# Requesting w_xo's last loads ahead of the expert weights, and a new order of the router's steps, in a hybrid mLSTM, attention and MoE block

## The chip, the cores and the metric

The kernel runs on one core of one Trainium2 chip. Its time is the device time of one execution in microseconds, taken as the median of several runs. A profiled execution gives a trace beside it: for each engine (TensorE, called PE here, with its weight loads PEld; VectorE, DVE; ScalarE, ACT; GpSimd, POOL; SyncE, SP, which issues most DMAs) when each instruction ran and what it waited for.

## What is computed

One block of a hybrid model on 512 tokens of width 1024, all in fp32: a mixer (mLSTM heads and forgetting attention, merged through `w_out`), a cross attention to 256 memory rows, and a mixture of 32 experts in four groups of which each token takes two. The change sits where the cross attention ends and the router begins:

```python
o = jnp.einsum('bhsn,bnhd->bshd', p.astype(v.dtype), v)
x = x + o.reshape(B, S, D) @ w_xo                  # residual 2
t = rmsnorm(x, g_moe)
g_logits = t @ w_rg + b_rg                         # 4 groups
e_logits = (t @ w_re + b_re).reshape(-1, N_GROUPS, EXPERTS_PER_GROUP)
# group by argmax, two experts in it by top_k, weights by softmax
for e in range(N_EXPERTS):
    he = jax.nn.silu(t @ w_gate[e]) * (t @ w_up[e])
    y = y + combine[:, e:e + 1] * (he @ w_down[e])
x = x + y
return rmsnorm(x, g_final)
```

## The kernel before

Every fp32 product of the dense part is made of three fp32r products (`mm3`, L102 to L105): an operand is split into a high part (ScalarE's copy, `wh`, L124) and a low part (VectorE's difference, `wl`, L125). `load_w` (L111) requests 512 KB of weights on SP into one of three buffers `wraw` and emits both halves of the split.

The product with `w_xo` is made in four column blocks of 256 (`resid_rows`, L522). The first two run beside the last head of the cross attention. The last two, `rw2` and `rw3` (L663), run token block by token block in the router's stretch: `of_block(tb)` (L181) makes the 24 products of one block of 128 tokens (12 with the weights' rows 0 to 511, 12 with the rest) and VectorE adds them to the residual (L525). In the order string below such a block is called `x0` to `x3` (for `rw2`) or `p0` to `p3` (for `rw3`). Each column block needs two loads, so the stretch has four.

The router's steps have letters too, and a token block behind them. `t` turns half a token block of the residual on PE (stage 0: columns 0 to 511; stage 1: the rest) and copies it out of PSUM (`rsc`); `l` multiplies it with the router's weights (`pso`, 40 columns); `s` and `r` sum the squares (ACT, L770) and take the power on POOL (L99); `X` writes the scaled residual in two fp16 parts, the high one on ACT (L783), the low one on DVE (L784); `g` scales the logits (`lg`, L790); `C` chooses the experts for two blocks (some 14 small DVE operations, from L799 to `ab`, L820); `K` counts places in three or seven small products (L829) and a chain on DVE; `G` gathers the first pair's tokens (L885). After that the experts run in 16 pairs: gate and up (L1045), turn (L1058), down (L1069), combine (L1095).

What sets the order: on PE, DVE and ACT the string `ROUT` (L46) is followed to the letter in this stretch (`manual_schedule`, L664); each of these engines works its instructions in order. SP and POOL are not in that list; their order is made by the scheduler of the framework. Expert weights are requested in 1 MB pieces in a ring of buffers (`RING`, L42): nine `m`, one `h` and one `l` (which share the buffers of w_xo's split halves and so wait for block p3) and three `r`. `experts.load(9)` requests the first nine, `experts.load(NAHEAD)` two more.

The weights' two last loads are requested at two places: `rw3.load(0)` ahead of `experts.load(9)` (L666), `rw3.load(4)` at the string's letter `v` (L671), which stood first in it.

Of the kernel before, what the change touches and what calls it, by code (L numbers as in the profile page):

```python
# [15 lines left out]
AF = mybir.ActivationFunctionType  # L16
OP = mybir.AluOpType
# [5 lines left out]
NB = T // P  # L23
# [19 lines left out]
NAHEAD = 11  # L43


ROUT = ("v x0 t00 t01 s0 l00 p0 t02 l01 t03 s1 r0 x1 l02 t10 X0 l03 p1 l10 r1 s2 x2 t11 X1 s3 g0 l11 g1 C0 p2 r2 x3 t12 "  # L46
        "X2 K0 l12 g2 p3 t13 r3 l13 g3 C1 G0 K1 X3 G1")
NR = 8 + NE

C_MLQ, C_MLK, C_MLV, C_MLO = 0, 512, 1024, 2048  # L50
# [8 lines left out]
def emit(ctx, tc, a):  # L59
    nc = tc.nc  # L60
    V, S, G, TE, SP = nc.vector, nc.scalar, nc.gpsimd, nc.tensor, nc.sync
# [66 lines left out]
    def drain(g):  # L128
        for _ in g:
            pass  # L130
# [367 lines left out]
    X1 = [X1a[:, tb] for tb in range(NB)]  # L498
# [17 lines left out]
    r2 = ExitStack()  # L516
# [5 lines left out]
    def resid_rows(src, hs, hl_, c):  # L522
        def ev(tb, n, ps):
            x = X1a[:, tb:tb + n, c * 256:(c + 1) * 256]
            V.tensor_add(x, x, ps)  # L525
        return Rows(src, c * 256, hs, hl_, NB, ev)
# [45 lines left out]
    xh = [XH[:, k] for k in range(KB)]  # L572
    xl = [XL[:, k] for k in range(KB)]
# [89 lines left out]
    rw2, rw3 = (resid_rows(a["w_xo"], oth, otl, c) for c in (2, 3))  # L663
    with tc.manual_schedule(engines={mybir.EngineType.PE, mybir.EngineType.DVE, mybir.EngineType.Activation}):  # L664
        rw2.loads()
        rw3.ws = [rw3.load(0)]  # L666
        experts.load(9)
        for w in ROUT.split():
            n = [int(x) for x in w[1:]]
            if w == "v":  # L670
                rw3.ws.append(rw3.load(4))  # L671
                experts.load(NAHEAD)
            elif w[0] in "xp":
                drain((rw2 if w[0] == "x" else rw3).of_block(n[0]))
            else:
                router[w[0]](*n)
# [48 lines left out]
def moe(ctx, tc, a, X2, dram, small, acc, pss, pso, left, right, ident, rpow, wp, c, mraw, wx):  # L725
    nc = tc.nc
    V, S, G, TE, SP = nc.vector, nc.scalar, nc.gpsimd, nc.tensor, nc.sync
# [14 lines left out]
    sq, lgs, m8s, ids = {}, {}, {}, {}  # L742
# [4 lines left out]
    def turn(stage, tb):  # L747

        pt = pss()
        for j, k in enumerate(range(*READY[stage])):  # L750
            TE.transpose(pt[:, j * P:(j + 1) * P], X2[tb][:, k * P:(k + 1) * P], ident)
        t = tTs[stage, tb] = wx.tile([P, 4, P], F32, name="rsc", tag="rsc", bufs=2)
        ptv = pt.rearrange("p (j t) -> p j t", j=4)
        if (stage, tb) == (1, NB - 1):
            V.tensor_copy(t, ptv)
        else:
            S.activation(t, ptv, AF.Copy)

    lp = []

# [15 lines left out]
        V.tensor_scalar(v, v, 1.0 / (D * XS * XS), None, op0=OP.mult)  # L776
        sq[tb] = rpow(v)

    def parts(tb):

        xh, xl = (c.XN[:, i, tb].rearrange("p (j q) -> p j q", j=KB) for i in range(2))
        xv = X2[tb].rearrange("p (q j) -> p j q", j=KB)
        S.activation(xh, xv, AF.Copy, scale=sq[tb][:, 0:1])  # L783
        V.scalar_tensor_tensor(xl, xv, sq[tb][:, 0:1], xh, op0=OP.mult, op1=OP.subtract)  # L784

    def scaled(tb):
        h, i = tb // 2, tb % 2
# [89 lines left out]
    def first(h):  # L877
# [3 lines left out]
        for i in range(4):  # L881
            for g, pt in enumerate(c.pts):
                for j in range(4):
                    tb, k = 2 * h + i // 2, 4 * g + j
                    TE.matmul(pt[:, j * P:(j + 1) * P], c.XN[:, i % 2, tb, k * P:(k + 1) * P], c.G0[:, tb],  # L885
                              start=h + i + j == 0, stop=h == 1 and i + j == 6, skip_group_check=True)

    router = dict(G=first, X=parts, C=choose, K=place, t=turn, l=logits, s=squares, r=rstd, g=scaled)
    c.codes, c.numbers = codes, numbers
    experts = Experts(ctx, tc, a, X2, dram, small, acc, pss, pso, left, right, ident, rpow, wp, c, mraw)  # L890
# [395 lines left out]
```

## Time and profile before

| | us |
|---|---|
| median of 3 runs | 1322.14 |
| lowest and highest | 1318.31, 1324.91 |
| the profiled execution | 1318.45 |
| its span, from the first to the last instruction | 1316.7 |
| PE busy in the span | 1252.7 (95%) |
| DVE, ACT, POOL busy | 553.1, 355.1, 131.9 |
| mean granted TensorE clock | 0.984 of full speed |
| router's stretch, from the end of block x0 to the first expert product | 750 to 823 |
| experts, to the end of the last pair's gate and up | 823 to 1287 |

The profile's page gives the time that each engine is busy, the chain of work that ended last (followed back from the last instruction to whatever released it), and groups of instructions. The trace answers with rows for a stretch: a timeline of one engine (start, length, line, operation, tile, and in brackets how long the engine was idle before it and what ended that), tables of stretches, and the waits by who waited for whom. The granted clock is a share of 2.4 GHz; its lower level is 0.50, 1.2 GHz. Engine time that waits for nobody's need costs nothing, so a share of busy time over the whole span says little about one stretch.

### The profile page before, as it was taken

The page shows a single profiled execution, that of the slowest core. Times are in us where ns is not written, and L with a number is a line of the kernel's source. Part 1 is how long each engine was busy: PE and PEld are TensorE (multiplying, and loading weights), DVE is VectorE, ACT ScalarE, POOL GpSimd, SP SyncE. Part 2 cuts the span into 40 slices and gives each one's busy share as a digit, 9 for nine tenths or more (in the row PEclk, how much of TensorE's full clock was granted, in tenths as well). Part 3 has the DMA queues.
Part 4 walks back from the last instruction along what each step waited for, and adds up shares of the span by engine and source line. Part 5 has one row for each costly group of instructions (what it writes and reads, how often), then busy time and mean ns, then how long its engine had stood idle before and what let it go on. Part 6 is the DMA issues. An engine that isn't in the chain of part 4 may idle for free.

```text
span 1316.7 us, 18633 instructions
## 1 busy us (share of the span) xinstructions
PE 1252.7 (95%) x7606; PEld 902.3 (69%) x7606; DVE 553.1 (42%) x1046; ACT 355.1 (27%) x626; POOL 131.9 (10%) x250
## 2 busy tenths in 40 slices
PE   6999999999999999999999867999999999999996
PEld 5898999888888977899978756444444444444443
DVE  5436455234565645447455326232232322222225
ACT  5335344223343433326334233010000000000102
POOL 0002010000001000001000002211111221111001
PEclk9999999999999999999999977999999999999998
DMA  4343432344254225324412614899999999999981
GB/s 167 86 106 88 78 99 74 96 82 103 74 94 84 78 96 160 111 98 149 162 49 64 270 66 176 343 418 418 418 417 417 419 417 417 414 416 417 419 333 65
DMA packets 99114, 278.45 MB, mean 211 GB/s; under 512 B 6197, under 2 KB 67909, under 8 KB 77905
## 3 DMA queue, kind: packets, MB, share of 16 engines
q1 hardware_dynamic: 97536, 272.46, 57.5%
q0 software_dynamic: 1488, 4.76, 1.1%
q8 instruction: 61, 1.00, 0.3%
q14 instruction: 29, 0.23, 0.0%
HBM read 275.08 MB, written 2.12 MB: 211 GB/s over the span
## 4 chain that ended last, share of the span: by engine, by line
PE 90%; DVE 3%; DMA 3%; ACT 1%; issue 1%; SPq 0%; POOL 0%; POOLq 0%; ACTq 0%; DVEq 0%
PE acc L1045 17%; PE acc L103 16%; PE acc L105 16%; PE acc L104 16%; PE pso L1069 8%; PE pss L1020 4%; DMA wraw<-w_xo 1%; PE pss L1095 1%; PE pso L1096 1%; PE pso L1095 1%; PE pss L103 1%; PE pss L105 1%; PE pss L104 1%; PE pss L1058 1%; PE pss L1096 1%
## 5 line engine op out<-in xcount | busy, mean ns | idle before, releaser
L1045 PE MATMUL acc<-mw,st 128*64 128x512 f32 x880 | 235.8, 598 | 0.6 <-DVE st L1022 0.6
L125 DVE TENSOR_TENSOR wl<-wraw,wh 128x1024 fp32r<-128x1024 f32 x120 | 146.8, 1224 | 200.0 <-ACT wh L124 195.5
L124 ACT ACTIVATE wh<-wraw 128x1024 fp32r<-128x1024 f32 x120 | 126.8, 1058 | 209.3 <-PE acc L104 91.0
L1045 PEld LDWEIGHTS acc<-mw,st 128*64 128x64 f32 x880 | 67.2, 136 | 108.2 <-issue 102.8
L103 PE MATMUL acc<-hH,wh 128*128 128x512 f32 x320 | 127.8, 399 | 0.0
L104 PE MATMUL acc<-hL,wh 128*128 128x512 f32 x320 | 127.2, 397 | 0.0
L105 PE MATMUL acc<-hH,wl 128*128 128x512 f32 x320 | 125.3, 399 | 1.7 <-DVE wl L125 1.7
L1080 DVE SCALAR_TENSOR_TENSOR yl<-pso,wsl,yh 128x512 fp32r<-128x512 f32 x32 | 22.6, 746 | 225.3 <-ACT yh L1079 225.3
L1069 PE MATMUL pso<-mw,hT 128*64 128x512 f32 x440 | 112.6, 592 | 0.7 <-ACT hT L1060 0.7
L104 PE MATMUL acc<-wl,hH 128*128 128x256 f32 x384 | 109.1, 285 | 1.0 <-DVE wl L125 1.0
L103 PE MATMUL acc<-wh,hH 128*128 128x256 f32 x384 | 109.3, 286 | 0.5 <-ACT wh L124 0.5
L105 PE MATMUL acc<-wh,hL 128*128 128x256 f32 x384 | 109.1, 285 | 0.2 <-DVE hL L196 0.2
L1031 POOL TENSOR_SCALAR G<-iot,code 128x64 f16<-128x64 f32 x120 | 52.7, 466 | 318.0 <-PE pss L1020 312.7
L1069 PEld LDWEIGHTS pso<-mw,hT 128*64 128x64 f32 x440 | 37.2, 137 | 61.4 <-issue 59.2
L104 PEld LDWEIGHTS acc<-wl,hH 128*128 128x128 f32 x384 | 73.1, 191 | 1.9 <-DVE wl L125 1.5
L103 PEld LDWEIGHTS acc<-wh,hH 128*128 128x128 f32 x384 | 72.7, 190 | 1.3 <-ACT wh L124 0.9
L105 PEld LDWEIGHTS acc<-wh,hL 128*128 128x128 f32 x384 | 73.0, 190 | 0.5 <-DVE hL L196 0.4
L105 PEld LDWEIGHTS acc<-hH,wl 128*128 128x128 f32 x320 | 60.2, 188 | 15.8 <-DVE wl L125 2.2
L103 PEld LDWEIGHTS acc<-hH,wh 128*128 128x128 f32 x320 | 60.3, 188 | 13.3 <-ACT wh L124 0.4
L104 PEld LDWEIGHTS acc<-hL,wh 128*128 128x128 f32 x320 | 60.3, 188 | 13.2
L1020 PEld LDWEIGHTS <-xn 128*128 128x128 f16 x960 | 53.7, 98 | 22.7 <-issue 22.7
L1079 ACT ACTIVATE yh<-pso,wsl 128x512 fp32r<-128x512 f32 x32 | 20.2, 683 | 154.1 <-PE pso L1069 154.1
(321 smaller groups left out, 2352.6 us busy)
## 6 DMA issues: line engine op xcount, KB each, us to landing
mw<-w_gate SPq DMA_DIRECT2D x55, 1024.0 KB, 14.4
mw<-w_up SPq DMA_DIRECT2D x55, 1024.0 KB, 13.4
mw<-w_down SPq DMA_DIRECT2D x55, 1024.0 KB, 11.8
wraw<-w_in SPq DMA_DIRECT2D x64, 512.0 KB, 5.2
wraw<-w_xkv SPq DMA_DIRECT2D x16, 512.0 KB, 3.4
mwl<-w_gate SPq DMA_DIRECT2D x10, 512.0 KB, 10.1
mwh<-w_up SPq DMA_DIRECT2D x10, 512.0 KB, 10.5
mwh<-w_down SPq DMA_DIRECT2D x10, 512.0 KB, 11.8
```

What stands on the lines that cost most here:

```text
L103: TE.matmul(out, ah, bh, start=start, stop=False, **kw)
L104: TE.matmul(out, ah, bl, start=False, stop=False, **kw)
L105: TE.matmul(out, al, bh, start=False, stop=stop, **kw)
L124: S.activation(h, raw, AF.Copy)
L125: V.tensor_sub(l, raw, h.bitcast(F32))
L1020: TE.matmul(pt[:, j * n:(j + 1) * n], c.XN[:, i % 2, i // 2, (4 * g + j) * P:(4 * g + j + 1) * P], G_[:, i // 2, :n], start=i == 0, stop=i ...
L1031: G.tensor_scalar(G_[:, tb, i * 64:i * 64 + 64], iot[:, :64], c.code[:, tb, e:e + 1], None, op0=OP.is_equal)
L1045: TE.matmul(ps[i][half(h)], sts[k // 4][:, k % 4, half(h)], w[i][k], start=k == 0, stop=k == KB - 1)
L1069: TE.matmul(o[n][half(h)], hT[:, j, half(h)], w[j][:, n * 512:(n + 1) * 512], start=j == 0, stop=j == 3)
L1080: V.scalar_tensor_tensor(yl[:k, c], o[n][:k], wcol, yh[:k, c].bitcast(F32), op0=OP.mult, op1=OP.subtract)
L1095: TE.matmul(o, C[:k, ts], yh[:k, c], start=True, stop=False)
L1096: TE.matmul(o, C[:k, ts], yl[:k, c], start=False, stop=True)
```

## The change

All four loads of `rw2` and `rw3` are now called for ahead of `experts.load(9)`, and the letter `v` stands behind x0 and two turns and requests expert pieces alone. In `ROUT` a block of products stands between the block whose residual a turn needs and that turn, and another between a turn and its logits; the chain g0, g1, C0 stands behind p2, l11 and r2; X2 and X3 are cut in their ACT half (`h`) and their DVE half (`l`), with K0 and p3, or K1, between the halves. The copy of the last turn (`t13`), which DVE made, goes to ACT like the others.

```diff
--- before.py
+++ after.py
@@ -43,8 +43,8 @@
 NAHEAD = 11
 
 
-ROUT = ("v x0 t00 t01 s0 l00 p0 t02 l01 t03 s1 r0 x1 l02 t10 X0 l03 p1 l10 r1 s2 x2 t11 X1 s3 g0 l11 g1 C0 p2 r2 x3 t12 "
-        "X2 K0 l12 g2 p3 t13 r3 l13 g3 C1 G0 K1 X3 G1")
+ROUT = ("x0 t00 t01 v s0 p0 l00 t02 s1 r0 x1 l01 t03 X0 p1 t10 l02 s2 r1 x2 l03 l10 t11 X1 s3 p2 l11 r2 g0 g1 C0 x3 t12 "
+        "X2h K0 p3 X2l l12 t13 r3 l13 g2 g3 C1 G0 X3h K1 X3l G1")
 NR = 8 + NE
 
 C_MLQ, C_MLK, C_MLV, C_MLO = 0, 512, 1024, 2048
@@ -663,12 +663,11 @@
     rw2, rw3 = (resid_rows(a["w_xo"], oth, otl, c) for c in (2, 3))
     with tc.manual_schedule(engines={mybir.EngineType.PE, mybir.EngineType.DVE, mybir.EngineType.Activation}):
         rw2.loads()
-        rw3.ws = [rw3.load(0)]
+        rw3.loads()
         experts.load(9)
         for w in ROUT.split():
-            n = [int(x) for x in w[1:]]
+            n = [int(x) if x.isdigit() else x for x in w[1:]]
             if w == "v":
-                rw3.ws.append(rw3.load(4))
                 experts.load(NAHEAD)
             elif w[0] in "xp":
                 drain((rw2 if w[0] == "x" else rw3).of_block(n[0]))
@@ -751,10 +750,7 @@
             TE.transpose(pt[:, j * P:(j + 1) * P], X2[tb][:, k * P:(k + 1) * P], ident)
         t = tTs[stage, tb] = wx.tile([P, 4, P], F32, name="rsc", tag="rsc", bufs=2)
         ptv = pt.rearrange("p (j t) -> p j t", j=4)
-        if (stage, tb) == (1, NB - 1):
-            V.tensor_copy(t, ptv)
-        else:
-            S.activation(t, ptv, AF.Copy)
+        S.activation(t, ptv, AF.Copy)
 
     lp = []
 
@@ -776,12 +772,14 @@
         V.tensor_scalar(v, v, 1.0 / (D * XS * XS), None, op0=OP.mult)
         sq[tb] = rpow(v)
 
-    def parts(tb):
+    def parts(tb, which="hl"):
 
         xh, xl = (c.XN[:, i, tb].rearrange("p (j q) -> p j q", j=KB) for i in range(2))
         xv = X2[tb].rearrange("p (q j) -> p j q", j=KB)
-        S.activation(xh, xv, AF.Copy, scale=sq[tb][:, 0:1])
-        V.scalar_tensor_tensor(xl, xv, sq[tb][:, 0:1], xh, op0=OP.mult, op1=OP.subtract)
+        if "h" in which:
+            S.activation(xh, xv, AF.Copy, scale=sq[tb][:, 0:1])
+        if "l" in which:
+            V.scalar_tensor_tensor(xl, xv, sq[tb][:, 0:1], xh, op0=OP.mult, op1=OP.subtract)
 
     def scaled(tb):
         h, i = tb // 2, tb % 2
```

Where instructions stand in the built programs, before and after, is shown at three places.

On SP, around w_xo's last load (`wraw_7239` before, `wraw_7221` after; the `mw` are 1 MB pieces of expert weights). Before:

```order
L116 DMA wraw_7215<-w_xo 128x4x256
L931 DMA mw_7221<-w_gate 128x2048
L931 DMA mw_7223<-w_up 128x2048
L931 DMA mw_7225<-w_gate 128x2048
L931 DMA mw_7227<-w_up 128x2048
L931 DMA mw_7229<-w_up 128x2048
L931 DMA mw_7231<-w_gate 128x2048
L931 DMA mw_7233<-w_up 128x2048
L931 DMA mw_7235<-w_gate 128x2048
L931 DMA mw_7237<-w_gate 128x2048
L116 DMA wraw_7239<-w_xo 128x4x256
```

Nine pieces of the experts stand ahead of it. After, on the same engine:

```order
L116 DMA wraw_7215<-w_xo 128x4x256
L929 DMA mw_7227<-w_gate 128x2048
L929 DMA mw_7229<-w_up 128x2048
L929 DMA mw_7231<-w_gate 128x2048
L929 DMA mw_7233<-w_up 128x2048
L929 DMA mw_7235<-w_up 128x2048
L929 DMA mw_7237<-w_gate 128x2048
L116 DMA wraw_7221<-w_xo 128x4x256
L929 DMA mw_7239<-w_up 128x2048
L929 DMA mw_7241<-w_gate 128x2048
L929 DMA mw_7243<-w_gate 128x2048
```

The last w_xo load has moved up past three of the nine pieces; six are still ahead of it.

On PE, around turn t11 (`pss`) and the logits (`pso`), between the end of block x2 and the start of block p2; minus is before, plus is after:

```order
 L104 MATMUL acc<-wl,oth_5687 128x256
 L105 MATMUL acc<-wh,otl_5688 128x256
-L751 MATMUL pss<-ident,x_4532 128x128 x4
-L766 MATMUL pso<-wr,rsc 128x40 x4
+L762 MATMUL pso<-wr,rsc 128x40 x8
+L750 MATMUL pss<-ident,x_4532 128x128 x4
 L103 MATMUL acc<-wh,oth_5673 128x256
 L104 MATMUL acc<-wl,oth_5673 128x256
```

Before, t11 is followed at once by its own logits l11; after, l03 and l10 come first, then t11, and l11 stands behind the block of products.

On DVE, around the residual add of block p3 (L525), behind the last hit of K0 (`G`). Before:

```order
L735 SCALAR_TENSOR_TENSOR G_5666<-iot,cd,GA 128x128
L790 SCALAR_TENSOR_TENSOR lg<-pso,rpow,br 128x40
L525 TENSOR_TENSOR x_4532<-x_4532,acc 128x256
L755 COPY rsc<-pss 128x512
L775 TENSOR_SCALAR vv<-ss 128x1
L776 TENSOR_SCALAR vv<-vv 128x1
L790 SCALAR_TENSOR_TENSOR lg<-pso,rpow,br 128x40
```

After, at the same place:

```order
L734 SCALAR_TENSOR_TENSOR G_5666<-iot,cd,GA 128x128
L525 TENSOR_TENSOR x_4532<-x_4532,acc 128x256
L782 SCALAR_TENSOR_TENSOR xn_7195<-x_4532,rpow,xn_7195 128x1024
L771 TENSOR_SCALAR vv<-ss 128x1
L772 TENSOR_SCALAR vv<-vv 128x1
L788 SCALAR_TENSOR_TENSOR lg<-pso,rpow,br 128x40 x2
```

X2's low half (`xn`), which stood ahead of K0's chain, now stands behind p3's add; the copy of t13 has left the engine, and both scalings g2 and g3 stand together.

## Rows read from the trace of the kernel before

**Rows 1.** The page, the chain that ended last, by engine.

```profile
PE 90%; DVE 3%; DMA 3%; ACT 1%; issue 1%; SPq 0%; POOL 0%; POOLq 0%; ACTq 0%; DVEq 0%
```

**Rows 2.** The chain row by row, experts: start us, length us, what.

```profile
902.63 3.58 PE acc L1045 x16
...
932.81 3.58 PE acc L1045 x16
```

**Rows 3.** Table of stretches: us, busy PE PEld DVE ACT POOL, PEclk, DMA share, GB/s.

```profile
750.20:766.10 15.90, 1.10 (x10) 0.86 (x9) 0.49 (x1) 1.58 (x3) 0.00 (x0) 0.60 0.78 316
766.10:770.47 4.37, 4.36 (x20) 4.36 (x21) 1.06 (x2) 1.05 (x3) 0.00 (x0) 0.50 0.00 0
...
790.94:797.77 6.83, 6.82 (x32) 6.83 (x33) 2.97 (x21) 1.45 (x8) 0.00 (x0) 0.50 0.00 0
...
822.90:1287.00 464.10, 460.09 (x2770) 204.74 (x2772) 130.82 (x221) 36.88 (x60) 71.17 (x129) 1.00 0.98 403
```

**Rows 4.** The chain row by row, router's stretch.

```profile
764.52 1.06 ACT wh L124
...
786.44 2.12 ACT xn L783
788.58 2.05 DVE xn L784
...
822.90 0.64 PE acc L1045
```

**Rows 5.** Timeline of SP: start us, us, engine, line, operation, tile.

```profile
739.30 0.50 SPq L931 DMA_DIRECT2D mw<-w_gate  x1
739.85 0.49 SPq L931 DMA_DIRECT2D mw<-w_up  x1
...
742.98 0.33 SPq L931 DMA_DIRECT2D mw<-w_gate  x1
745.52 0.38 SPq L116 DMA_DIRECT2D wraw<-w_xo  x1
...
804.52 0.33 SPq L936 DMA_DIRECT2D mwl<-w_gate  x1
```

**Rows 6.** DMA issues, sixth and ninth expert piece: KB, us to landing.

```profile
mw<-w_gate SPq DMA_DIRECT2D x1, 1024.0 KB, 16.2
...
mw<-w_gate SPq DMA_DIRECT2D x1, 1024.0 KB, 20.1
```

**Rows 7.** Timeline of PE: start us, us, line, tile, [idle before <-releaser].

```profile
766.11 1.93 PE L766 MATMUL pso<-wr,rsc 128*128 128x40 f32 x8 [14.81 <-ACT rsc L757]
...
773.57 0.36 PE L103 MATMUL acc<-wh,oth 128*128 128x256 f32 x1
...
776.52 0.98 PE L766 MATMUL pso<-wr,rsc 128*128 128x40 f32 x8
777.33 0.63 PE L751 MATMUL pss<-ident,x 128*128 128x128 f32 x4
...
790.95 1.90 PE L766 MATMUL pso<-wr,rsc 128*128 128x40 f32 x8 [5.05 <-DVE lg L790]
...
802.02 1.08 PE L766 MATMUL pso<-wr,rsc 128*128 128x40 f32 x8 [0.62 <-ACT rsc L757]
...
809.25 0.44 PE L751 MATMUL pss<-ident,x 128*128 128x128 f32 x2 [2.99 <-DVE x L525]
```

**Rows 8.** Timeline of DVE: step r1, then scaling g1 and the end of C0.

```profile
784.14 0.21 DVE L775 TENSOR_SCALAR vv<-ss 128x1 f32<-128x1 f32 x1 [0.79 <-ACT xn L770]
...
792.89 0.26 DVE L790 SCALAR_TENSOR_TENSOR lg<-pso,rpow,br 128x40 f32<-128x40 f32 x1 [2.09 <-PE pso L766]
...
795.98 0.19 DVE L820 TENSOR_TENSOR ab<-eb 128x64 bf16<-128x64 bf16 x1
```

**Rows 9.** Waits of SP's queue, of PE in experts: us, times, longest.

```profile
SPq L931 <- PE acc L1045: 214.1, 52, 14.1
...
PEld acc L1045 <- DMA mw<-w_down: 1.2, 4, 0.4
```

## The prediction

> **What bounds the kernel now.** I read the page's chain of waits first: TensorE (PE) holds 90% of it [rows 1]. In the chain row by row, the experts' stretch repeats: the same step of two neighbouring pairs stands at 902.63 and 932.81 us, 30.18 us apart, and nothing but PE lies between [rows 2]. That stretch, 822.9 to 1287 us, has PE busy 460.1 of 464.1 us at full clock and moves 403 GB/s [rows 3]. The change leaves its instructions and their order alone; it can only start earlier or later. So the question is when the first expert product runs (822.90 us, [rows 4]), and the stretch to read is the router's, from 750 us on.
>
> There PE is not the bound. In the table of stretches it is busy 1.1 us of 15.9 us from 750.2 to 766.1, and after this gap the granted clock is 0.50 (1.2 GHz) until 770.47; after a second gap it is 0.50 again from 790.94 to 797.77 [rows 3]. The PE timeline says what each gap waits for: 14.81 us for ScalarE's copy (rsc) of the first turn, 5.05 us for VectorE's scaled logits (lg, L790), 0.62 us for a copy, 2.99 us for the residual add of p3 [rows 7]. The first is no fault of the copy. ScalarE works in order, and ahead of the copy stands the split of w_xo's last load, which starts at 764.52 [rows 4]. That load was issued at 745.52 behind nine 1 MB loads of expert weights [rows 5].
>
> **Part 1, the load.** The words say "ahead of the experts' loads"; the built order says otherwise. On SP the last w_xo load now stands behind six expert loads in place of nine. The sixth was issued at 739.30 and landed 16.2 us later, at 755.5; the ninth was issued at 742.98 and landed 20.1 us later, at 763.1 [rows 5, 6]. So 7.6 us separate them, 2.5 us for each MB, and landings come in the order of the requests. Before, the split began 1.4 us after the ninth landing; the same distance behind the sixth is 757.0. Bounds: 755.5 (no distance at all) and 759.5 (as late as the expert load behind it, plus the distance). I take 757.0, since both loads are of one size and shape and stand in one queue. SP issues it at about 739.9, where the seventh expert load went [rows 5]; the three expert loads that it now precedes get 0.5 MB later, and nobody needs them before 830 us.
>
> The Trainium skill (DMA: Bandwidth & Descriptors, section "Queues, rings and completion order") says that on each DMA engine requests are taken in ring order, but that completion is not first in, first out for the issuing engine. By the first half the load waits for six; by the second it could land early, which is my third rival. The landings read here are in order.
>
> With the split at 757.0 and 1.06 us long [rows 4], the high half is there at 758.1. PE meanwhile runs more than before: x0, two turns, and now half of block p0 (the 12 products of w_xo's rows 0 to 511, already split), since p0 no longer stands behind the first logits. A 24-product block takes 776.52 - 773.57 = 2.95 us at full clock [rows 7], so half is 1.5. PE resumes at 758.1, 8.0 us earlier than 766.11, with 1.5 us done; then it waits about 1.1 us for the low half on VectorE, which follows the high half. Head: 8.0 + 1.5 - 1.1 = **8.4 us** gained (bounds 6 to 10 with the landing).
>
> **Part 2, logits and turns.** (a) The 5.05 us wait stood at l11, whose PSUM tile g0 reads; g0 waited behind both halves of parts X1 (2.12 us on ScalarE from 786.44, 2.05 us on VectorE from 788.58 [rows 4]). Now l11 stands ahead of g0 and has block p2 between its turn and itself: 2.95 us cover the turn's copy. **5.05** gained. The 0.62 us in front of l12 goes for the same reason: **0.6**.
>
> (b) What is late next is K0, whose three products need the end of C0. From turn t11 on, X1 takes 0.6 (copy) + 2.1 + 2.05 us, then p2's add 0.4, r2 (0.8 until the square is there, two small operations 0.4), g0 0.2, and g1 with C0, which ran from 792.89 to 796.17, 3.3 us [rows 8]: about 10 us after t11. PE has p2, l11, x3 and t12 in that time: 2.95 + 0.8 + 2.95 + 0.5 = 7.2 us; 0.8 is 777.33 less 776.52, a set of logits [rows 7]. A new wait of about 3 us, which I take as **-3.1** with the products' way to VectorE and back. Behind it queue p3, l12 and t13.
>
> (c) The 2.99 us before t13: PE had ended p3 by 806.26 (809.25 less 2.99), yet p3's add was done only at about 809.2 [rows 7], because X2's low half and K0's chain stood ahead of it on VectorE. In the new order the low half stands behind that add, and l12 (0.8 us) covers the add's 0.4 and the way to it. The wait goes and l12 has moved under cover: **3.4** gained. In return r3's small operations stand behind X2's low half and come 0.6 to 0.9 us later into g3, and t13's copy goes to ScalarE, 0.6 us for VectorE's 0.7, which alters nothing: **-0.8**.
>
> (d) The clock. Before, 4.36 + 6.82 us of PE's work ran at 0.50 [rows 3]; at full clock it would have taken half, so 5.6 us were lost. After, the head's gap shrinks from 14.8 to 5.6 us but still is longer than the 5.05 us after which the clock fell, so the first products run at 1.2 GHz, and more of them: the rest of p0, l00, t02 and part of x1. From 758.1 I put the rise, as after the first gap (4.4 us) or the second (6.8 us), between 763 and 767; I take 7.9 us of work, 4.0 us lost. Net **+1.6**, bounds -1 and +4. Here the skill (TensorE: Matmul & The Clock Gate, "What's actually happening") adds that the activity monitor runs freely and doesn't restart with the kernel, so this term may differ from run to run; no view here can show that.
>
> **Sum.** 8.4 + 5.05 + 0.6 - 3.1 + 3.4 - 0.8 + 1.6 = 15.2 us, bounds 10 and 19. The tail behind it (C1, G0, K1, X3, G1) keeps its order on VectorE; splitting X3 and X2 in two names moves no further ScalarE work past another engine's need. Everything from 822.90 on moves along: SP waits for PE's products to free a buffer, 214.1 us in 52 waits, and PE's waits for weights are at most 0.4 us [rows 9], so the loads are released by PE and come earlier with it. The profiled execution took 1318.45 us (span 1316.7): it would be 1303.2. The median of the runs is 3.7 us higher, 1322.14, and the spread 1318.31 to 1324.91; less 15.2 that is **1307 us**.
>
> **Rivals.**
> 1. The gap at K0 drops the clock as the 5.05 us gap did. For: it is about 3 us long, with little work just ahead of it. Against: after the 2.99 us gap at 809.25 the next logits did not slow at once. Price: block p3 at half speed, at most another 2.95 us: 1310 us.
> 2. The load comes no earlier: it shares the queue with the loads behind it, and its 1 KB rows are served late. Then 7.6 us of the head stay: 1314.7 us. For: before, it was the last in the queue and had no company. Against: the landings are in order.
> 3. It does what its words say, the load landing among the w_xo loads at about 743. Then nothing waits at the head: 14.8 in place of 8.4, and no slow stretch there, 4 us more: 1297 us. Against: the built order of SP.
> 4. Slower: the experts' loads can't follow. The loads that wait for p3's products (804.52 on SP [rows 5]) precede the first expert product by 18.4 us; about 17 are left, for some 5 MB at 2.5 us each. If PE overtakes the weights, it waits in each pair, and the stretch behind each wait runs at 1.2 GHz: one 16-product stretch (3.58 us [rows 2]) in 14 pairs is 50 us, 1357 us. It decides as soon as PE's waits for weights exceed about 1 us a pair; today they are 0.4 at most, so I give it little.
>
> **How the numbers follow.** The forecast, 1304 to 1310, has 0.60; rival 1 0.15; rival 2 0.08; rival 3 0.07; rival 4 0.03; 0.07 is left for things between. The range 1300 to 1313.5 takes the forecast, rival 1, the landing's bounds and the runs' spread of some 3 us, and leaves out rivals 2, 3 and 4, 0.18 together. A difference under 0.5% (6.6 us) can't be told from no change: 0.90 faster, 0.07 the same (half of rival 2 and a forecast whose small terms all fail), 0.03 slower.
>
> **What would show it.** Right: w_xo's last split starts near 757; PE's first gap is near 5.6 us and comes inside p0, not ahead of l00; no wait of logits for lg; a new wait of some 3 us at the products of place K0; no wait of t13 for the add; the first expert product near 807.5; the pairs still 30.18 us apart. Wrong: the split near 743 or 764, a half-clock stretch behind K0, or waits for mw tiles in the experts.

## The result, and the profile after

| | before | after |
|---|---|---|
| median of 4 runs, us | 1322.31 | 1304.53 |
| lowest and highest | 1318.31, 1324.91 | 1304.21, 1306.05 |
| the profiled execution | 1318.45 | 1306.05 |
| its span | 1316.7 | 1304.3 |
| forecast | | 1307 (1300 to 1313.5) |

The ratio is 0.987, with an interval of 0.9844 to 0.9897, all of it below 1: faster, as forecast, though by less than 2%. The medians differ by 17.8 us where 15.2 were forecast. Between the two profiled executions it is 12.4. The sum was worked out on one profiled execution and subtracted from a median, so this gap between 12.4 and 17.8 has to be explained too.

The chain of the profile after, by engine, answers to [rows 1]; two rows of it, from the experts, to [rows 2] (start us, length us, what):

```profile
PE 91%; DVE 4%; DMA 2%; ACT 1%; issue 1%; SPq 1%; POOL 0%; POOLq 0%; ACTq 0%; DVEq 0%
```

```profile
890.15 3.58 PE acc L1043 x16
...
920.33 3.58 PE acc L1043 x16
```

The pairs are still 30.18 us apart. PE's waits for weights in the experts (us, times, longest) are as small as before [rows 9]:

```profile
PEld acc L1043 <- DMA mw<-w_up: 0.9, 3, 0.3
```

So from these pairs on the experts came earlier as one block (their first products did not, see below), and rival 4 (their loads can't follow) is out. The router's stretch, ScalarE and then PE (start us, us, line, tile, in brackets the idle time before and what ended it), answers to [rows 4, 7]:

```profile
757.44 1.06 ACT L124 ACTIVATE wh<-wraw 128x1024 fp32r<-128x1024 f32 x1 [13.79 <-DMA wraw<-w_xo]
```

```profile
758.55 0.58 PE L103 MATMUL acc<-wh,oth 128*128 128x256 f32 x1 [5.19 <-ACT wh L124]
759.81 0.58 PE L104 MATMUL acc<-wl,oth 128*128 128x256 f32 x1 [0.68 <-DVE wl L125]
...
789.92 0.18 PE L827 MATMUL pso<-ab,before 128*128 128x32 bf16 x1 [3.05 <-DVE ab L818]
...
792.92 0.98 PE L762 MATMUL pso<-wr,rsc 128*128 128x40 f32 x8
...
795.06 1.09 PE L762 MATMUL pso<-wr,rsc 128*128 128x40 f32 x8 [0.69 <-ACT rsc L753]
795.97 1.96 PE L883 MATMUL pss<-G,xn 128*128 128x128 f16 x32
...
800.12 0.18 PE L827 MATMUL pso<-ab,before 128*128 128x32 bf16 x1 [2.15 <-DVE ab L818]
...
803.62 2.72 PE L883 MATMUL pss<-G,xn 128*128 128x128 f16 x24 [3.22 <-DVE G L734]
806.87 1.04 PE L883 MATMUL pss<-G,xn 128*128 128x128 f16 x8 [0.52 <-DVE xn L782]
808.26 7.53 PE L1043 MATMUL acc<-mw,st 128*64 128x512 f32 x24 [0.36 <-DVE st L1020]
```

These are all of PE's waits between x0 and the experts. The split starts at 757.44, the gap comes inside p0 and is 5.19 us long, the waits for `lg` and for p3's add are gone, place K0 has its new wait of 3.05. One wait was not in the forecast: 2.15 us at place K1. The first expert product runs at 808.26, not 807.5, and with its 23 followers takes 7.53 us, where the same 24 took 5.37 before. The table of stretches (us, busy PE PEld DVE ACT POOL, granted clock, DMA share, GB/s) answers to [rows 3]:

```profile
758.55:768.20 9.65, 8.97 (x41) 8.68 (x42) 2.33 (x5) 3.35 (x9) 0.55 (x1) 0.50 0.46 192
768.20:797.97 29.77, 26.04 (x242) 25.54 (x242) 16.43 (x57) 15.16 (x27) 2.24 (x4) 1.00 0.17 54
...
803.62:808.26 4.64, 3.76 (x33) 3.23 (x32) 3.94 (x7) 0.00 (x0) 4.64 (x7) 0.50 0.97 408
```

The clock stays at 2.4 GHz over the wait at K0 and through p3, so rival 1 did not happen in this execution. It is at 1.2 GHz behind the first gap and again at 803.62, after PE had waited 2.15 and 3.22 us with little work between.

### The profile page after: what moved, and what is told of

Same layout as the page of the kernel before. It is cut to its first block, busy times and chain, and to the rows that moved or that the text cites. A ratio compares the mean times of both kernels' runs of the same rounds, so it can differ in the third digit from the quotient of the medians.

```text
span 1304.3 us, 18633 instructions
## 1 busy us (share of the span) xinstructions
PE 1253.0 (96%) x7606; PEld 900.9 (69%) x7606; DVE 552.6 (42%) x1045; ACT 355.7 (27%) x627; POOL 132.3 (10%) x250
## 4 chain that ended last, share of the span: by engine, by line
PE 91%; DVE 4%; DMA 2%; ACT 1%; issue 1%; SPq 1%; POOL 0%; POOLq 0%; ACTq 0%; DVEq 0%
PE acc L1043 18%; PE acc L103 16%; PE acc L104 16%; PE acc L105 16%; PE pso L1067 8%; PE pss L1018 4%; PE pss L1093 1%; DMA wraw<-w_xo 1%; PE pso L1094 1%; PE pso L1093 1%; PE pss L103 1%; DVE wl L125 1%; PE pss L105 1%; PE pss L104 1%; PE pss L1056 1%
```

## The experiments

### One part of the change alone

e_order keeps the new order of the steps and puts the load back behind nine pieces; e_load keeps the old order and moves the load alone.

```diff
(e_order, against the changed kernel)
-        rw3.loads()
+        rw3.ws = [rw3.load(0)]
         experts.load(9)
+        rw3.ws.append(rw3.load(4))
...
(e_load, against the kernel before)
-        rw3.ws = [rw3.load(0)]
+        rw3.loads()
...
-                rw3.ws.append(rw3.load(4))
```

> The changed kernel with one thing undone: w_xo's last load is requested behind nine expert pieces again (as before), all steps of the router stay in the new order. Theory (the two parts add up): the last split starts near 764.5 us in place of 757.4, PE's gap inside p0 grows from 5.2 to some 12.3 us, and everything behind it moves by 7.1 us: about 1311.6 us, first expert product near 815.4. Rival A (the load hardly matters, since VectorE's chain sets the end of the stretch): some of the 7.1 us come back before the first expert product, 1304 to 1307 us. Rival B (the order brings nothing without the load): about 1320 us.

> The kernel before with one thing changed: w_xo's last load is requested behind six expert pieces in place of nine, the router's steps stay in the old order. Theory: the last split starts near 757 us, PE's gap of 14.8 us shrinks by 7.5, and the waits of 5.05, 0.62 and 2.99 us stay: about 1314.7 us, first expert product near 815.4. Rival A (the load hardly matters): 1320 us or more. Rival B (the load is the whole of the change): 1305 us.

| | median, us | ratio to before, interval | saved |
|---|---|---|---|
| e_order | 1311.98 (5 runs) | 0.9933 (0.9912 to 0.9954) | 10.3 |
| e_load | 1314.80 (6 runs) | 0.9943 (0.9924 to 0.9962) | 7.5 |
| both, the change | 1304.53 (4 runs) | 0.987 (0.9844 to 0.9897) | 17.8 |

Saved is counted from 1322.31. 10.3 + 7.5 = 17.8, and both rivals of each expectation fall. That the sum is exact is chance, since the runs of e_order spread over 3.2 us and those of e_load over 5. The traces add up too: from the end of x0 (the start of turn t00) to the first expert product it is 74.11 us in a second profile of the kernel before (r_before, below), 67.12 in e_load, 64.68 in e_order and 57.37 in the changed kernel. The load alone saves 7.0, the order alone 9.4, both 16.7. The first gap of PE in the two profiles, e_order and then e_load:

```profile
763.55 0.58 PE L103 MATMUL acc<-wh,oth 128*128 128x256 f32 x1 [12.75 <-ACT wh L124]
```

```profile
758.60 1.93 PE L765 MATMUL pso<-wr,rsc 128*128 128x40 f32 x8 [7.22 <-ACT rsc L756]
```

Three expert pieces ahead of the load cost 12.75 - 5.19 = 7.6 us in the new order and 14.81 - 7.22 = 7.6 in the old, 2.5 us a piece, as read from the landings [rows 5, 6].

### The load truly first

Six pieces still stood ahead of it. SP had to wait there for one of three `wraw` buffers, and since SP's order is the framework's to make, it put expert pieces ahead; that the wait was its reason is argued, not shown. e_first holds SP to the written order.

```diff
-    with tc.manual_schedule(engines={mybir.EngineType.PE, mybir.EngineType.DVE, mybir.EngineType.Activation}):
+    with tc.manual_schedule(engines={mybir.EngineType.PE, mybir.EngineType.DVE, mybir.EngineType.Activation, mybir.EngineType.SP}):
         rw2.loads()
```

> The changed kernel, with SP's instructions held to the written order too, so that all loads of w_xo stand ahead of every expert piece; SP then waits for a buffer until about 739.4 us and requests the expert pieces some 3 us later. Theory: the load lands near 743.5 us, the gap of 5.2 + 0.7 us inside p0 goes, the stretch at 1.2 GHz from 758.5 to 768.2 (some 4.8 us lost) goes with it: 10 us less than the changed kernel, 1294 us; experts' weights still land 25 us ahead of use. Rival A: PE only reaches the wait at place K0 earlier, since VectorE's and ScalarE's chains don't get faster; that wait grows from 3 to 6 us: 1298 us. Rival B: the expert pieces that come 3 us later are missed later: PE waits for weights, 1305 us or more.

1294.66 us (4 runs), ratio 0.98 (0.9775 to 0.9825): 9.9 us less than the changed kernel, 10 expected. The load's issue (KB, us to landing), in the changed kernel and then in e_first:

```profile
wraw<-w_xo SPq DMA_DIRECT2D x1, 512.0 KB, 17.4
```

```profile
wraw<-w_xo SPq DMA_DIRECT2D x1, 512.0 KB, 3.4
```

The same half megabyte takes 17.4 us behind six pieces and 3.4 us with none ahead. SP stands still for it, and the first piece goes out later:

```profile
735.53 3.56 SPq L116 DMA_DIRECT2D wraw<-w_xo  x2
739.15 0.50 SPq L929 DMA_DIRECT2D mw<-w_gate  x1
```

That is 739.15 in place of 736.62, and its use is at 798.52; PE's waits for weights stay at 0.3 us at most, so rival B falls. Rival A falls too: the wait at K0 is 3.04 us as before. The stretches show where the 10 us were: the gaps of 5.19 and 0.68 us and 9 us of work at half speed (4.5 us lost) are gone, 10.4 us in all; p3 and the logits behind it, slower by 1.5 us, take part of it back. From x0's end to the first expert product it is 48.29 us, 9.1 less than in the changed kernel. The profiled executions differ by more, 11.9 us, mostly because the first 24 expert products took 5.37 us here.

```profile
747.56:778.80 31.24, 28.21 (x244) 28.03 (x243) 12.82 (x39) 16.38 (x28) 1.64 (x3) 1.00 0.53 222
778.80:782.96 4.16, 4.16 (x27) 4.16 (x27) 2.61 (x11) 0.99 (x7) 0.58 (x1) 0.69 0.40 92
...
784.33:798.52 14.19, 7.05 (x84) 6.21 (x82) 11.90 (x46) 5.98 (x13) 6.73 (x9) 0.76 0.92 352
```

The second row is what rival 1 of the prediction had described: behind the same wait at K0, 3.04 us, the clock did fall here, and K0's products with p3 took 4.16 us where the changed kernel had 3.0 (789.92 to 792.92).

### Single steps of the order

Three changes to the changed kernel's order string, of which the parts that move are shown; the second also gives t13's copy back to VectorE:

```diff
(e_l11)
-t11 X1 s3 p2 l11 r2 g0 g1 C0 x3 t12
+t11 X1 s3 g0 l11 g1 C0 p2 r2 x3 t12
(e_x2)
-X2h K0 p3 X2l l12
+X2 K0 p3 l12
-        S.activation(t, ptv, AF.Copy)
+        if (stage, tb) == (1, NB - 1):
+            V.tensor_copy(t, ptv)
+        else:
+            S.activation(t, ptv, AF.Copy)
(e_k0)
-X2h K0 p3 X2l l12
+X2h p3 K0 X2l l12
```

> The changed kernel with one reordering undone: l11 stands behind turn t11 and g0 again, and block p2 behind C0, as before. Theory (terms a and b of the sum): the wait of l11 for VectorE's scaled logits comes back (5.0 us) and the wait at place K0 (3.05 us) goes, so PE reaches p3 2.0 us later and all behind it too: 1306.5 us; if the clock falls behind that gap as it did in the kernel before, up to 3.4 us more. Rival A: C0, K0 and the tail come earlier by as much as p2 comes later, and the time stays at 1304.5. Rival B: the reordering was worth its 5.05 us whole: 1309.5 us.

> The changed kernel with the part on X2 and t13 undone: X2's low half stands ahead of K0's chain on VectorE again, and VectorE copies t13. By the prediction (3.4 less 0.8) this costs 2.6 us: 1307.1 us. Theory after seeing the trace: the add of p3 comes 1.4 us later and PE waits for it at t13, but r3's small operations no longer stand behind X2's low half, so the scaled logits g3, which set the end, come only some 0.8 us later: 1305.3 us. Rival: the add that comes later moves everything behind it by the 3 us that t13 waited in the kernel before: 1307.5 us.

> The changed kernel with K0's three products moved behind block p3, which fills PE's wait of 3.05 us at place K0. Theory: behind p3 VectorE's chain (add of p3, K0's chain, X2's low half, g3, C1, K1's chain, X3's low half: some 15 us of work in a row) sets the end, so PE's 3 us come back as other waits and the first expert product moves by less than 1 us: 1304 us. Rival: PE's waits add up to the end, and the time falls by the whole 3 us to 1301.5 us.

e_l11: 1306.95 us (4 runs), 2.4 more than the changed kernel, 2.0 expected. The wait of l11 is back with 5.11 us, that at K0 is gone; putting p2 ahead was worth the difference and not the 5.05 us that the row in the kernel before shows. Both rivals fall.

```profile
781.57 1.90 PE L762 MATMUL pso<-wr,rsc 128*128 128x40 f32 x8 [5.11 <-DVE lg L788]
```

In the trace the first expert product comes 51.66 us after PE's resumption, 1.95 later than the 49.71 of the changed kernel, and 5.11 - 3.05 is 2.06. The clock did fall behind this wait, but it had risen earlier behind the first gap (some 4.4 us at half speed in place of 9.7); that the two cancel is luck.

e_x2: 1305.92 us (4 runs, 1303.7 to 1306.83), 1.4 more than the changed kernel. In the traces the first expert product comes 50.37 us after PE's resumption (759.13 to 809.50), against 49.71 (758.55 to 808.26): 0.7. The wait that returns at t13 is small:

```profile
795.53 0.44 PE L750 MATMUL pss<-ident,x 128*128 128x128 f32 x2 [0.97 <-DVE x L525]
```

The medians lie between 0.8 and 2.6 and their runs are scattered over 3 us, so they decide little; the trace speaks for the 0.8 and against the 2.6 of the prediction.

e_k0: 1304.50 us (4 runs, 1300.84 to 1305.46), as much as the changed kernel. The wait at K0 is gone (0.23 us are left), and nothing came of it in the median: VectorE's chain is the bound from there on. In the changed kernel VectorE is busy 13.1 of the 15.3 us from p3's end to the first expert product, PE 8.4. The profiled run of e_k0, 1300.84, is not typical; the next part says why.

### What scatters the runs

The runs of one kernel differ by 2 to 7 us. So both kernels were profiled once more, unchanged; and e_warm fills the tail's idle PE time with products that nobody reads.

```diff
+    def warm(n):
+        pw = pso()
+        for _ in range(n):
+            TE.matmul(pw, c.XN[:, 0, 0, :P], c.XN[:, 0, 1, :512], start=True, stop=True)
...
-l13 g2 g3 C1 G0 X3h K1 X3l G1
+l13 g2 g3 C1 G0 W8 X3h K1 W14 X3l G1
...
```

> The kernel before once more, unchanged. Theory: its runs (1317.8 to 1324.9 us) differ by when the clock falls and rises, not by any wait: the waits of 14.8, 5.05 and 2.99 us stand as before within 0.3 us, and where the time is above 1320 us, the stretches at 1.2 GHz are longer (the first 24 expert products take 7.5 us, or the products behind the first gap run slow for longer). Rival: the load lands at another time (split 3 us later or more), and the clock is the same.

> The changed kernel once more, unchanged. Theory: 1304.5 us within 1.5; the waits stand as in the first profile within 0.5 us, and the difference to it is in the stretches at 1.2 GHz (the rise behind the first gap at 768.2 us or up to 5 us earlier; the first 24 expert products in 7.5 or 5.4 us). Rival: the waits themselves differ.

> The changed kernel with idle PE time filled: 8 and 14 products of 512 columns that nobody reads are added, the first lot behind the first gather (where PE waits 2.15 us at place K1), the second behind K1's products (where PE waits 3.2 us). Theory: the first 24 expert products took 7.53 us at 808.26 in place of 5.37 because the clock had fallen over these gaps; with the gaps filled they take 5.4 us, and the time falls by about 2 us, to 1302.5 us, if the filling does not itself delay the last gather. Rival: the first products are slow for another reason (their weights, the tile st): they stay at 7.5 us, and the time stays at 1304.5 us or rises by up to 2 us.

r_before took 1322.56 us, 4.1 more than the first profiled execution of the same program. r_after took 1306.22, 0.2 above what was expected at most (1304.5 within 1.5); its waits stand as in the first profile within 0.1 us. Lines of r_before (PE):

```profile
766.27 1.93 PE L766 MATMUL pso<-wr,rsc 128*128 128x40 f32 x8 [14.56 <-ACT rsc L757]
...
791.37 1.90 PE L766 MATMUL pso<-wr,rsc 128*128 128x40 f32 x8 [5.04 <-DVE lg L790]
...
809.81 0.69 PE L751 MATMUL pss<-ident,x 128*128 128x128 f32 x2 [3.00 <-DVE x L525]
811.29 1.93 PE L766 MATMUL pso<-wr,rsc 128*128 128x40 f32 x8 [0.78 <-DVE rsc L755]
...
824.78 7.58 PE L1045 MATMUL acc<-mw,st 128*64 128x512 f32 x24 [0.36 <-DVE st L1022]
```

The waits are those of [rows 7] within 0.3 us, but for 0.40 us at K1 that came with the slower logits. The work is not: the last logits take 1.93 us where the first execution had 1.08, and the first 24 expert products 7.58 where it had 5.37. That execution's rows:

```profile
810.47 1.08 PE L766 MATMUL pso<-wr,rsc 128*128 128x40 f32 x8 [0.78 <-DVE rsc L755]
811.39 3.58 PE L885 MATMUL pss<-G,xn 128*128 128x128 f16 x32
...
822.90 5.37 PE L1045 MATMUL acc<-mw,st 128*64 128x512 f32 x24 [0.56 <-DVE st L1022]
```

In the tail of r_before the granted clock is 0.61 on the mean, in that of the first execution 0.75, over the same steps (r_before, then before):

```profile
809.80:824.78 14.98, 9.68 (x82) 8.59 (x82) 10.98 (x45) 5.61 (x12) 6.90 (x10) 0.61 0.80 327
```

```profile
809.25:822.90 13.65, 8.57 (x81) 7.76 (x81) 10.96 (x45) 5.56 (x12) 6.68 (x9) 0.75 0.88 358
```

So the clock's timing alone moved this kernel by 1.3 + 2.2 us. Of the other 0.6, some 0.4 are slow stretches behind the first two waits that last a little longer (15 of the 128x256 products at half speed behind the first, where it was 12), and 0.2 stand already where PE resumes (766.27 against 766.11); x0's later end, 0.4 us, went mostly into that wait, 14.56 us for 14.81. With the same waits ahead of them (2.15 at K1 in the new order, 1.70 in e_x2; 3.22; 0.52), the first 24 products took 7.53 (after), 7.37 (r_after), 7.43 (e_order), 7.46 (e_l11), 7.00 (e_x2), and 5.37 in e_first. e_k0's run of 1300.84 had luck twice: those 24 products in 5.37 us, and full clock 5 us after the first gap instead of 9.7:

```profile
758.44:763.40 4.96, 4.28 (x19) 3.99 (x19) 1.95 (x3) 1.53 (x4) 0.00 (x0) 0.50 0.82 339
763.40:787.69 24.29, 24.06 (x208) 23.95 (x207) 10.10 (x35) 13.69 (x22) 2.23 (x4) 1.00 0.04 11
```

In e_warm the clock holds through the tail, and the 24 products run at full speed:

```profile
800.90:804.40 3.50, 3.31 (x19) 1.49 (x19) 3.11 (x15) 1.54 (x3) 1.70 (x3) 1.00 1.05 437
804.40:808.82 4.42, 2.28 (x32) 1.81 (x31) 3.93 (x7) 0.00 (x0) 4.42 (x6) 1.00 0.98 408
808.82:814.19 5.37, 5.37 (x26) 1.70 (x27) 0.54 (x1) 0.00 (x0) 3.46 (x9) 1.00 0.22 56
```

The 5.37 alone would not prove it, since e_first had it without filling; but there the clock over the tail was 0.76 on the mean and here it is 1.00. So the rival, slow for their weights or for `st`, falls. The median did not show the 2 us: 1304.27 us (4 runs, 1303.5 to 1306.68). Two profiled runs in which x0 ends at the same 751.36 do show it, 1304.45 in e_warm against 1306.22 in r_after, but that is one run of each. Whether a filling pays here stays open.

Not all of the scatter is explained. Part of it arises ahead of the stretch that the edits touch: x0 ends at 748.34 in e_order's profile, at 749.42 in e_l11's, and between 750.2 and 751.4 in all others. In those two the granted clock is 1.00 throughout from 500 to 700 us; in each of the others it is 0.98 over either 500 to 600 or 600 to 700. And the four runs of e_x2 range from 1303.7 to 1306.83 us with the same mean clock, 0.988, so there the clock's mean doesn't tell the runs apart.

### A faster version

From e_first on, three steps, each added to the one ahead: b_tail puts the VectorE operations for the later pairs' token numbers (`codes`, `numbers`) behind the first `st` tiles; b_best puts X1's low half behind p2's add; b_best2 puts K0 behind p3.

```diff
(b_tail: one hand-made order for st, the first six steps of the first pair, codes and numbers)
             sts = [stationary(c.G0, g, pt=c.pts[g]) for g in range(2)]
+            ps = [acc(), acc()]
+            gu = gate_up(sts, [(ex.rows(e, 0), ex.rows(e, 1)) for e in (0, 1)], ps)
+            advance(gu, 6)
+            for f in (c.codes, c.numbers):
+                for h in range(2):
+                    f(h)
+            weight_parts()
...
(b_best)
-t11 X1 s3 p2 l11 r2
+t11 X1h s3 p2 X1l l11 r2
(b_best2)
-X2h K0 p3 X2l l12
+X2h p3 K0 X2l l12
```

> The kernel with all loads of w_xo first (the one of the earlier run with SP in the written order), with one more change: the eight VectorE operations that prepare the token numbers and codes of the later pairs (jk, code, R, Vj), which stand ahead of X3's low half, are put behind the two st tiles of the first pair. Theory: VectorE's chain sets the end there, and these take some 2.4 us of the 4.4 us between K1's products and X3's low half; the first expert product comes 2.4 us earlier: 1292.3 us against 1294.7. Rival: the products that need Vj and R (behind the first 24 expert products) then wait as long, or the second pair's tokens come too late on GpSimd: 1294.7 us or more.

> The kernel with all loads of w_xo first and the token numbers behind st, with one more change: X1's low half on VectorE stands behind the add of p2, as X2's low half stands behind that of p3. Theory: the add of p2 waited 2.2 us for X1's low half, and r2's squares on ScalarE (0.7 us) hide behind X1's low half instead; C0 and the wait at place K0 come 0.9 us earlier: 1291.6 us. Rival: VectorE's chain is as long as before, nothing moves: 1292.5 us.

> The kernel of b_best, and K0's products behind block p3. Theory: PE's wait of some 2 us at place K0 goes and VectorE's chain becomes the only bound from there: 0.5 us less than b_best, 1291 us. Rival: the add of p3 then comes no earlier relative to VectorE's chain and K0's chain delays X2's low half and r3: no gain or up to 1 us more than b_best.

| | median of 4 runs, us | lowest and highest | ratio to before, interval |
|---|---|---|---|
| b_tail | 1292.54 | 1291.36, 1295.07 | 0.9795 (0.9768 to 0.9822) |
| b_best | 1291.59 | 1290.12, 1291.99 | 0.9766 (0.9750 to 0.9783) |
| b_best2 | 1289.77 | 1288.61, 1291.24 | 0.9749 (0.9732 to 0.9765) |

b_tail gave 2.1 us (2.4 expected; in the traces the first expert product moves by 3.05, but some 1.5 of that is e_first's slow p3 with the logits behind it), b_best 1.0 (0.9), b_best2 1.8 (0.5). The intervals of neighbouring steps overlap, so the size of a single step rests on the traces: from x0's end to the first expert product it is 48.29 us in e_first, then 45.03, 44.09 and 43.83, so that b_best's step is 0.9 and b_best2's 0.3. From K1's products to the first expert product e_first needed 798.52 - 790.55 = 8.0 us; in b_best2, with nothing but K1's own chain and X3's low half between, it is 6.2:

```profile
788.93 0.18 PE L827 MATMUL pso<-ab,before 128*128 128x32 bf16 x1 [4.19 <-DVE ab L818]
...
791.21 3.59 PE L883 MATMUL pss<-G,xn 128*128 128x128 f16 x32 [2.00 <-DVE G L734]
795.16 5.81 PE L1043 MATMUL acc<-mw,st 128*64 128x512 f32 x24 [0.36 <-DVE st L1020]
```

PE's wait at K1 has grown to 4.19 us while the time fell: in this tail a wait of PE says where VectorE's chain is, not what can be gained. b_best2 beats both kernels: 14.8 us less than the changed one.

## Why the prediction was right, and where it was off

**The terms.** Both profiled executions, from x0's end to p3's end and on to the first expert product, close the sum:

| term | forecast | measured | from |
|---|---|---|---|
| head | 8.4 | 8.4 | 766.11 - 758.55, plus 1.5 for 12 products, less 0.68 |
| l11's wait | 5.05 | 5.05 | gone |
| l12's wait | 0.6 | 0.62 | gone |
| K0's new wait | -3.1 | -3.05 | 789.92 |
| t13, l12 under cover, r3 | 3.4 - 0.8 | 2.5 | p3's end to the first expert product 17.0 before (805.87 to 822.90), 15.3 after (792.92 to 808.26): 1.7; plus 0.8 for l12, which no longer stands ahead of p3. From the last logits to K1's products: 4.3 before (810.47 to 814.76), 5.1 after (795.06 to 800.12), which is the -0.8 |
| clock up to p3's end | 1.6 | 1.1 | at 0.50 before 4.36 + 6.82 us, after 8.97 us; half of each is lost |
| first expert product | 15.2 | 14.6 | 822.90 - 808.26 |

The load's place, read from the built order against the words of the change, and its landing, 757.0 against 757.44, carried the head; e_load and e_order confirm it apart from the rest. l11's wait and K0's go together: e_l11 shows that the 5.05 and the -3.1 are worth the 2 us between them. The row of t13 closes in the sum, but its reason is shown in part only: putting X2's low half and t13's copy back cost 0.7 us by e_x2's trace and 1.4 by its median, so the larger share of the 2.5 came with l12 and g2 behind p3, which no run took apart alone. Rivals 2 and 3 fall with 757.44; rival 1 did not happen in the changed kernel's two profiles (p3 ends 3.0 us after K0's start in both), but e_first shows that it can, at some 1.5 us with the logits behind p3. The prediction's argument against it, that the logits behind the 2.99 us gap did not slow, held for one execution alone: in r_before they took 1.93 us behind 3.00. What rival 3 priced, the load truly first at 1297 us, e_first did for 1294.66. The Trainium skill's remark that completion is not first in, first out (DMA: Bandwidth & Descriptors, "Queues, rings and completion order") leaves room for the load to land early; here it landed 17.4 us after its request, in its turn.

**What was off.** (1) The clock term. The rise behind the first gap was put between 763 and 767 and came at 768.2: 0.5 us. (2) The step "everything from 822.90 on moves along". From the first expert product to the end of the span it was 493.8 us before and 496.0 after: the clock had fallen by then, and the first 24 products took 2.16 us longer. The forecast gave no price to the clock at that place; it had looked for a fall only behind K0. (3) The unforeseen wait at K1. PE's work in the tail ran at full clock after (G0's 32 products in 1.96 us, before 3.58), and PE waited 2.15 us for C1 instead: PE's speed there was worth nothing, since VectorE set the tail. The totals did not suffer, as the term for that part was worked out on VectorE's order.

**The base.** 15.2 us were taken from a median of 1322.14, but worked out on an execution of 1318.45. r_before shows what lies between them: the same waits, a slower clock in the tail and in the first 24 products. Of like with like, r_before and r_after, the first expert product moves from 824.78 to 808.59, by 16.2 us, and the time by 16.3. So the usual run of before loses some 3.5 us to the clock that the profiled one didn't; the usual run of after has the slow 24 products as well, but not the slow last logits. Like with like the change is worth 16.3 us where 15.2 were forecast. Of the last 1.5 us to the 17.8 of the medians, 0.7 arise ahead of the change (x0 ends at 751.36 in r_after, at 750.67 in r_before); the rest lies within the scatter of the runs and is not settled.

Some of the closeness is luck. The forecast left out the slow first products of after, which cost 2.2 us, and the slower usual run of before, which adds 3.5; the two partly cancel. For the profiled execution it had said 1303.2, 2.9 us too low, and for the median 1307, 2.5 too high. The Trainium skill (TensorE: Matmul & The Clock Gate, "What's actually happening") holds that the activity monitor runs freely, and so that the point of change varies from run to run; the two traces of one program agree that it varies, with 5.37 and 7.58 us for the same 24 products behind waits that are the same within 0.4 us; they don't show why.

## What to carry to other kernels

A load that someone waits for must be looked up in the order that was built, not in the program's text: a bulk prefetch of megabytes ahead of it in one queue cost 2.5 us a piece here, and the prefetch had slipped ahead where the load's request had to wait for a buffer. Holding the issuing engine back for 2.5 us was worth 10, because the pieces had tens of microseconds to spare. Where one engine's chain sets a stretch, price moves on that engine: e_k0 removed a 3 us wait of PE and gained nothing, b_tail took operations off VectorE's chain and gained 2.1. And a forecast made on one execution should be compared with more than one: profile the kernel before a second time before its waits and its clock are added up.

## What the runs showed of the hardware

Not expected was how much of the scatter is the clock: two executions of one program with nearly equal waits differed by 4.1 us (1318.45 and 1322.56), and their mean granted clocks were 0.984 and 0.979. In the tail the last logits ran in 1.08 or 1.93 us, the first 24 expert products in 5.37 (before) to 7.65 us (e_load), and a wait of 3.04 us at K0 lowered the clock in e_first but not in r_after (nor one of 3.05 in the changed kernel's first profile). With PE's idle time filled by products that nobody reads the granted clock stayed at 1.00 (e_warm). In one queue on SP, 512 KB landed 17.4 us after the request behind six 1 MB loads and 3.4 us after it with none of them ahead.
